# A decoder layer's recurrence: the tiled output products of eight chunks in one visit instead of two, and the output transposes six dense products later

## The chip, the cores and the metric

One core of a Trainium2 chip runs the kernel. A core has TensorE (PE, with its weight loads PEld), VectorE (DVE), ScalarE (ACT), GpSimd (POOL) and SyncE (SP), which here issues most of the DMAs. The engines run their own instruction lists and wait for one another through semaphores. TensorE writes to PSUM, eight banks of 128 partitions by 512 fp32 columns; all else lies in SBUF or in DRAM. The metric is the device time in microseconds, the median of several runs.

## The reference

One layer (DEPTH is 1) of a decoder trunk over 512 tokens of width 2048, all fp32:

```python
h = rms_norm(x, norm_g[i])
z = jnp.einsum('btd,dn->btn', h, w_in[i])     # r, k, v, lora inputs | gate | pool input | pool gate
...
def step(S, inp):                              # per head, 64 x 64 state
    sa = jnp.einsum('bhvk,bhk->bhv', S, -kk_t)
    S = S * w_t + sa * (kk_t * a_t) + v_t * k_t
    y_t = jnp.einsum('bhvk,bhk->bhv', S, r_t)
...
y = head_group_norm(y, ln_w[i], ln_b[i])       # per head and token, over 64 values
y_rwkv = (y + bonus) * jax.nn.silu(g_rwkv)
...                                            # pooled half, concat
x = x + jnp.einsum('btc,cd->btd', y_mix, w_out[i])
x = x + jax.nn.sigmoid(x @ w_pg[i] + b_pg[i]) * (p[i] @ w_ple[i])
return rms_norm(x, final_g)
```

The change concerns `y_t` for the 16 heads, the group norm behind it and the order of work around them.

## The kernel before

The large products (input projections, output projection, gate) are dense: weights and activations are split into a high and a low fp32r part (`wsplit`, `split`, L127 to L139: ScalarE casts the high part, VectorE subtracts), and three 128x128 by 128x512 matmuls per block of the contraction (`mm3`) stand for one fp32 product.

The recurrence goes by pairs of heads, j = 0 to 7, a pair filling 128 partitions, and by chunks of 64 tokens, ch = 0 to 7. Within a chunk the recurrence is turned into small matrix products. `recur(j, ...)` (L753) walks the eight chunks. A chunk has three hops on TensorE, each waiting for the one before through another engine:

- `py` (L781): the state block `sbd` of the chunk's start times the chunk's queries. It gives the state's part of the outputs, in one half of the rows, and the part that the next hop needs, in the other; VectorE adds `mv` to that other half and writes `zs` (L784).
- `pu` (L790): the inverted triangular block `x1` times `zs`. ScalarE copies the result into `uv` (L794).
- `ps` (L799): the keys `bkn` times `uv`, from which VectorE makes the next state block `sbd` (L804, L806).

A tile `py` is one PSUM bank and holds four chunks. The outputs also need products within the chunk, masked scores `mt` times `uv`. These are the tiled products: 64 output rows, 64 columns, the two chunks of an even-odd couple going to the two halves of the rows. They are added onto `py` eight calls at a time, after chunk 3 and after chunk 7; each call is two matmul instructions in the trace, so a visit has 16. ScalarE then copies the outputs of the four chunks from the bank to `ysb` (L827, two copies of 64x256). VectorE computes the group norm's statistics over `ysb` (L842, L844), a reciprocal square root in small steps (`rsqrt`, L142), and scales (L851).

Between the hops TensorE is kept busy with dense products. A generator `stream()` (L461) yields the dense work of the whole stage in a fixed order; `pump(n)` (L492) takes about n matmuls from it. `HC = (6, 9, 9)` (L867) are the amounts behind `py`, `pu` and `ps`.

`finish` (L854) is the end of a pair: four transposes of `ysb` to `pyt` (L858), ScalarE's scale and bias to `yo` (L860), two VectorE steps (L861, L862) and one DMA to the DRAM tensor `yd` (L863), issued by ScalarE. `yd` is read when the output projection starts. `finish` of pair j is put on the list `pending` and called while the next pair is prepared, in `gather(j + 1)` (L678); that of the last pair is called behind a pump of 40 (L902).

`gather(j)` runs between two pairs: decay and rate products `pu`, `pa` (L528, L543), transposes of v (`pv`, L688) and of the keys (`pbk`, L699), a pump of 8, the key norms `pss` (`norm_key`, L563), then the pumps and `finish` that the change touches, then the second half of the inversion: VectorE's transposes to `y1` (L723), the reciprocal of the key norms behind them (L572), and on TensorE `pq2`, `pmv` and `px2` (L728 to L741; the trace calls them pq, pmv, px), whose result completes `x1` (L745) for the next pair's first `pu`.

`scores(j + 1)` (L608) is called after chunk 0 of pair j. Its products `pm` need `bk` and `ar`, which VectorE makes in `prepare` (L577).

What sets the order: on TensorE every instruction of this stage is kept in program order (`pin`, L154 to L162). On the other engines a planner orders the instructions by priority and estimated times; `tc.high_priority` lifts those of the recurrence's hops, and `tc.issue_after` puts some behind others.

PSUM pools: `psY` has two banks under tag `y`, used in turn by `pv`, by two of the four `pm` tiles and by the `py` tiles. `psM` has three banks, for `pu`/`pa` of `decay_and_rate`, `pbk`, `pss`, `pyt`, `pq2`, `pmv`, `px2` and others. `psA` holds the dense accumulations, `psS` the `pu` and `ps` of the hops.

Of the kernel before, what the change touches and what calls it, by code (L numbers as in the profile page):

```python
# [9 lines left out]
F32 = mybir.dt.float32  # L10
# [5 lines left out]
P = 128  # L16
T = 512
# [7 lines left out]
NCH = T // C  # L25
# [9 lines left out]
def trunk_kernel(ctx: ExitStack, tc: tile.TileContext, x, p, norm_g, w_in, mu, w0, w_up, a0, a_up,  # L35
                 k_k, k_a, r_k, ln_w, ln_b, w_pool, pool_scale, w_out, w_ple, w_pg, b_pg, final_g, out):
    nc = tc.nc
# [118 lines left out]
    def mm(*a, **k):  # L156
        i = nc.tensor.matmul(*a, **k)  # L157
        return tc.keep_in_program_order(i) if pin[0] else i
# [333 lines left out]
    def pump(n):  # L492
        debt[0] += n
        while debt[0] > 0:
            c = next(big, None)
            if c is None:
                debt[0] = 0
                return
            debt[0] -= c
# [178 lines left out]
    def gather(j):  # L678
        d = st_[j]
        bk, v_, mt = d.pop("bk"), d.pop("v_"), d["mt"]  # L680
        if j + 1 < NJ:
            prepare_key(j + 1)
            decay_and_rate(j + 1)

        uv = rw.tile([P, NCH, P], F32, name=f"uv{j}", tag="uv")
        ps = psY.tile([P, T], F32, name=f"pv{j}", tag="y")
        for tt in range(NT):
            tr(ps[:, tt * P:(tt + 1) * P], v_[:, tt * P:(tt + 1) * P], ident)  # L688
        pv = ps.rearrange("p (t c) -> p t c", c=P)
        nc.scalar.copy(uv[0:64, 0::2, :], pv[0:64])  # L690
        nc.scalar.copy(uv[64:128, 1::2, :], pv[64:128])


        bkn = rw.tile([P, NCH, P], F32, name=f"bkn{j}", tag="bkn")
        for hf in range(2):
            ps = psM.tile([P, T], F32, name=f"pbk{j}_{hf}", tag="m")
            for i in range(4):
                ch = 4 * hf + i
                tr(ps[:, i * P:(i + 1) * P], bk[:, ch // 2, 2 * (ch % 2):2 * (ch % 2) + 2, :], ident)  # L699
            nc.scalar.copy(bkn[:, 4 * hf:4 * hf + 4, :], ps.rearrange("p (c n) -> p c n", n=P))  # L700

        pump(H4)

        d.update(uv=uv, bkn=bkn)
        if j + 1 < NJ:
            norm_key(j + 1)
        pump(H5)
        if pending:
            pending.pop()()
        pump(HX)  # L710

        x1 = d["x1"]

        def units(fn):
            for u in range(8):
                for par in range(2):
                    fn(u, par, 64 * (1 - par))

        y1 = rw.tile([P, 8, 32], F32, name=f"y1{j}", tag="tm")

        with tc.issue_after(late[0].ins):
            for pb in (0, 64):
                yt = nc.vector.transpose(y1[pb:pb + 32], x1[pb:pb + 32, :, 0:32])  # L723
        if j + 1 < NJ:
            with tc.issue_after(yt.ins):
                scale_key(j + 1)
        ps3 = psM.tile([P, 8, 32], F32, name=f"pq2{j}", tag="m")
        units(lambda u, par, pb: mm(ps3[pb + 32:pb + 64, u, :],  # L728
                                                  mt[pb:pb + 32, par, u, 1 - par, 32:64],
                                                  y1[pb:pb + 32, u, :], start=True, stop=True,  # L730
                                                  tile_position=(pb, pb + 32)))
        q2t = rw.tile([P, 8, 32], F32, name=f"q2{j}", tag="xw")
        with tc.high_priority(offset=HP):
            for pb in (0, 64):
                nc.scalar.copy(q2t[pb + 32:pb + 64], ps3[pb + 32:pb + 64])
        psv = psM.tile([P, 8, C], F32, name=f"pmv{j}", tag="m")
        units(lambda u, par, pb: mm(psv[pb:pb + 64, u, :], mt[64 - pb:128 - pb, par, u, 1 - par, :],
                                    uv[64 - pb:128 - pb, 2 * (u // 2) + par, 64 * (u % 2):64 * (u % 2) + 64],
                                    start=True, stop=True))
        ps4 = psM.tile([P, 8, 32], F32, name=f"px2{j}", tag="m")  # L740
        units(lambda u, par, pb: mm(ps4[pb:pb + 32, u, :], q2t[pb + 32:pb + 64, u, :],  # L741
                                                  x1[pb + 32:pb + 64, u, 32:64], start=True, stop=True,
                                                  tile_position=(pb + 32, pb)))
        for pb in (0, 64):
            nc.scalar.copy(x1[pb:pb + 32, :, 32:64], ps4[pb:pb + 32])  # L745
        mv = rw.tile([P, 4, P], F32, name=f"mv{j}", tag="mv")
        nc.scalar.copy(zsp[0][64:128, :].rearrange("p (h t) -> p h t", h=2), psv[64:128, 0:2, :])
        nc.scalar.copy(mv.rearrange("p q (h t) -> p (q h) t", h=2), psv)
        d["mv"] = mv
        pump(2 * H1)  # L750


    def recur(j, work, between):  # L753
# [13 lines left out]


        ysb = rw.tile([P, NT, P], F32, name=f"ysb{j}", tag="t", bufs=4)
        py = None  # L770
        for ch in range(NCH):
            par, q = ch % 2, ch // 2
            pb = 64 * (1 - par)
            cur, nxt = sbd[ch % 2], sbd[(ch + 1) % 2]
            pcc = pw[:, ch, C:C + 1]
            sl = slice((ch % 4) * P, (ch % 4 + 1) * P)
            if ch % 4 == 0:
                py = psY.tile([P, T], F32, name=f"py{j}_{ch}", tag="y")
            zs = zsp[par]
            if ch > 0:  # L780
                mm(py[:, sl], ar[:, q, 2 * par:2 * par + 2, :], cur, start=ch in (1, 4), stop=True,  # L781
                                 skip_group_check=True)
                with tc.high_priority(offset=HP):
                    lead[0] = nc.vector.tensor_tensor(zs[pb:pb + 64], py[pb:pb + 64, sl], mv[pb:pb + 64, q, :],  # L784
                                                      ALU.add)
                step()
                pump(HC1)

            psu = psS.tile([P, T], F32, name=f"pu{j}_{ch}", tag="s")
            mm(psu[:, 0:P], x1[:, 2 * q:2 * q + 2, :], zs, start=True, stop=True)  # L790
            for h in range(2):
                hc = slice(64 * h, 64 * h + 64)
                with tc.high_priority(offset=HP):
                    nc.scalar.copy(uv[pb:pb + 64, ch, hc], psu[hc, hc])  # L794
            step()
            pump(HC2)
            if ch < NCH - 1:
                pss = psS.tile([P, T], F32, name=f"ps{j}_{ch}", tag="s")
                mm(pss[:, 0:P], bkn[:, ch, :], uv[:, ch, :], start=True, stop=True)  # L799
                for h in range(2):  # L800
                    hc = slice(64 * h, 64 * h + 64)
                    with tc.high_priority(offset=HP):
                        if ch == 0:
                            lead[0] = nc.vector.tensor_scalar(nxt[hc, hc], pss[hc, hc], pcc[hc], None, ALU.mult)  # L804
                        else:
                            lead[0] = nc.vector.scalar_tensor_tensor(nxt[hc, hc], pss[hc, hc], pcc[hc], s0p[hc, :],  # L806
                                                                     ALU.mult, ALU.add)
                s0p = rw.tile([P, C], F32, name=f"s0p{j}_{ch}", tag="s0p", bufs=2)
                pcn = pw[:, ch + 1, C:C + 1]
                if ch < NCH - 2:  # L810
                    for h in range(2):
                        hc = slice(64 * h, 64 * h + 64)
                        nc.gpsimd.tensor_scalar(s0p[hc, :], nxt[hc, hc], pcn[hc], None, ALU.mult)  # L813
            if ch % 4 == 3:
                for qq in range(2):
                    for h in range(2):
                        for pr in range(2):
                            c_ = ch - 3 + 2 * qq + pr
                            yr = slice(64 * pr, 64 * pr + 64)
                            o_ = (2 * qq + pr) * P + 64 * h  # L820
                            mm(py[yr, o_:o_ + 64], mt[:, pr, 2 * (c_ // 2) + h, pr, :],
                                             uv[:, c_, 64 * h:64 * h + 64], start=False, stop=True,
                                             skip_group_check=True)
                py4 = py.rearrange("p (s c) -> p s c", c=P)
                for pr in range(2):
                    yr = slice(64 * pr, 64 * pr + 64)
                    nc.scalar.copy(ysb[yr, q - 1:q + 1, :], py4[yr, pr::2, :])  # L827
            step()
            if ch == 0:
                between()  # L830
            else:
                pump(HC3)
# [345 lines left out]
```

## Time and profile before

| what | value |
|---|---|
| median of three runs | 1095.2 us (1094.84 to 1095.33) |
| the profiled execution: its own time, and its span | 1094.06 us, 1092.3 us |
| granted TensorE clock, mean | 0.998 |
| busy in the span: PE, PEld, DVE, ACT, POOL | 1067.4, 879.1, 707.9, 448.2, 74.4 us |
| busy from 125 to 715 us, which holds the eight recurrences | PE 585.7, DVE 448.2, ACT 248.7 of 590 us |
| tiled products mt times uv | 256 matmul instructions, 16 a visit, 16 visits from 155.7 to 699.5 us |
| ysb copies | 32, median 367 ns |

A row of the time line gives the start, the length in us, engine, line, operation, output and inputs, shapes, the count of instructions merged in the row, and in brackets the engine's idle time before it with what ended it. A row of the chain of waits gives start, length and what; the chain is followed back from the last instruction to what released it. A row of the waits gives who waited for whom: the total, the number of times and the longest. Of TensorE the matmuls overlap, so the start of the next row, not the length, tells what one costs. A row by stretch has the stretch, its length, then busy us and count of PE, PEld, DVE, ACT and POOL, the granted clock, the DMA share and the GB/s.

### The profile page before, as it was taken

Reading aid. Unit: us, or ns where it says so; the run is one execution under the profiler, and the core shown is the slowest. Engines: PE = TensorE matmul, PEld = TensorE weight load, DVE = VectorE, ACT = ScalarE, POOL = GpSimd, SP = SyncE. Lnnn points to the kernel's source line nnn. Section 1 sums busy time; section 2 is a strip of 40 time slices with the busy share of each in tenths; the row PEclk is TensorE's granted clock in tenths of the full one; section 3 lists DMA queues with packets and bytes.
Section 4 is the critical chain, followed back from the end, with each engine's and each line's share of the span. In section 5 each row is a group of like instructions: output and inputs, shape, how many; then the busy total and the mean of one; then the engine's idle time right before and its main releaser. Section 6 shows DMA issues by size and latency. Waiting matters only on the chain.

```text
span 1092.3 us, 17194 instructions
## 1 busy us (share of the span) xinstructions
PE 1067.4 (98%) x6060; PEld 879.1 (80%) x6060; DVE 707.9 (65%) x1835; ACT 448.2 (41%) x917; POOL 74.4 (7%) x180
## 2 busy tenths in 40 slices
PE   5999999999999999999999999999999999999996
PEld 4888878888888888787888788888888888888885
DVE  6687867878779679678886956454433424445366
ACT  7633534435335335353443344544222222233337
POOL 2100010110110110100101101000000000000000
PEclk9999999999999999999999999999999999999999
DMA  7433433332423333333334242774534438454534
GB/s 233 116 97 97 112 92 79 102 101 72 127 81 102 105 91 89 95 83 90 94 93 120 79 138 94 231 242 163 171 123 141 164 97 261 129 187 147 174 105 154
DMA packets 178485, 138.56 MB, mean 127 GB/s; under 512 B 34677, under 2 KB 139742, under 8 KB 178398
## 3 DMA queue, kind: packets, MB, share of 16 engines
q1 hardware_dynamic: 157694, 103.89, 32.2%
q10 hardware_dynamic: 20704, 33.56, 9.5%
q8 instruction: 48, 0.79, 0.3%
q14 instruction: 39, 0.32, 0.1%
HBM read 118.02 MB, written 18.87 MB: 125 GB/s over the span
## 4 chain that ended last, share of the span: by engine, by line
PE 88%; DVE 5%; DMA 3%; ACT 2%; issue 1%; SPq 0%; ACTq 0%; DVEq 0%
PE acc_o L157 16%; PE acc_g L157 16%; PE zb L157 15%; PE zv L157 8%; PE zr L157 7%; PE zg L157 7%; PE zk L157 6%; DMA n<-nd 2%; PE py L157 2%; PE pple L157 2%; PE pu L157 2%; PE pm L157 1%; PE pp L157 1%; PE ps L157 1%; PE pmv L157 1%
## 5 line engine op out<-in xcount | busy, mean ns | idle before, releaser
L133 DVE TENSOR_TENSOR wlo_g<-raw_g,whi_g 128x512 fp32r<-128x512 f32 x84 | 56.9, 683 | 78.7 <-ACT whi_g L132 78.5
L157 PE MATMUL zb<-hhi,whi_b 128*128 128x512 f32 x256 | 106.3, 415 | 0.0
L133 DVE TENSOR_TENSOR wlo_o<-raw_o,whi_o 128x512 fp32r<-128x512 f32 x64 | 43.9, 690 | 92.3 <-ACT whi_o L132 92.2
L157 PE MATMUL zb<-hhi,wlo_b 128*128 128x512 f32 x256 | 100.5, 393 | 0.0
L157 PE MATMUL acc_o<-whi_o,ylo 128*128 128x512 f32 x256 | 100.2, 391 | 0.0
L157 PE MATMUL acc_o<-whi_o,yhi 128*128 128x512 f32 x256 | 99.9, 390 | 0.0
L157 PE MATMUL zb<-hlo,whi_b 128*128 128x512 f32 x256 | 99.8, 390 | 0.0
L157 PE MATMUL acc_o<-wlo_o,yhi 128*128 128x512 f32 x256 | 99.7, 389 | 0.0
L132 ACT CAST whi_g<-raw_g 128x512 fp32r<-128x512 f32 x84 | 51.9, 620 | 105.5 <-PE acc_g L157 60.3
L157 PE MATMUL acc_g<-whi_g,x2hi 128*128 128x512 f32 x208 | 81.2, 391 | 0.0
L157 PE MATMUL acc_g<-wlo_g,x2hi 128*128 128x512 f32 x208 | 81.0, 389 | 0.0
L157 PE MATMUL acc_g<-whi_g,x2lo 128*128 128x512 f32 x208 | 80.6, 389 | 0.0
L132 ACT CAST whi_o<-raw_o 128x512 fp32r<-128x512 f32 x64 | 39.9, 623 | 97.8 <-PE acc_o L157 97.8
L813 POOL TENSOR_SCALAR s0p<-sbd,pw 64x64 f32<-64x64 f32 x96 | 56.7, 590 | 338.5 <-DVE sbd L806 253.7
L132 ACT CAST whi_b<-raw_b 128x512 fp32r<-128x512 f32 x64 | 39.7, 620 | 87.1 <-PE zv L157 34.9
L133 DVE TENSOR_TENSOR wlo_b<-raw_b,whi_b 128x512 fp32r<-128x512 f32 x64 | 43.7, 684 | 34.2 <-ACT whi_b L132 33.0
L157 PEld LDWEIGHTS zb<-hhi,wlo_b 128*128 128x128 f32 x256 | 48.0, 188 | 11.0
L661 DVE TENSOR_TENSOR xw<-xw,tm 128x60 f32<-128x60 f32 (+24 forms) x248 | 51.9, 209 | 6.8
L157 PEld LDWEIGHTS acc_o<-wlo_o,yhi 128*128 128x128 f32 x256 | 48.1, 188 | 10.0
L157 PEld LDWEIGHTS acc_o<-whi_o,ylo 128*128 128x128 f32 x256 | 48.1, 188 | 9.9
L157 PEld LDWEIGHTS acc_o<-whi_o,yhi 128*128 128x128 f32 x256 | 48.1, 188 | 9.6
L157 PEld LDWEIGHTS zb<-hhi,whi_b 128*128 128x128 f32 x256 | 48.3, 189 | 8.4
(285 smaller groups left out, 2546.8 us busy)
## 6 DMA issues: line engine op xcount, KB each, us to landing
raw_b<-in_w_in_dram SPq DMA_DIRECT2D x64, 256.0 KB
raw_o<-in_w_out_dram SPq DMA_DIRECT2D x64, 256.0 KB
raw_g<-in_w_pg_dram SPq DMA_DIRECT2D x64, 256.0 KB
raw_k<-in_w_in_dram SPq DMA_DIRECT2D x32, 256.0 KB
raw_r<-in_w_in_dram SPq DMA_DIRECT2D x32, 256.0 KB
raw_v<-in_w_in_dram SPq DMA_DIRECT2D x32, 256.0 KB
raw_g<-in_w_in_dram SPq DMA_DIRECT2D x32, 256.0 KB
n<-nd SPq DMA_DIRECT2D x16, 256.0 KB
```

What stands on the lines that cost most here:

```text
L132: nc.scalar.copy(hi, raw)
L133: nc.vector.tensor_tensor(lo, raw, hi.bitcast(F32), ALU.subtract)
L157: i = nc.tensor.matmul(*a, **k)
L661: nc.vector.tensor_tensor(xw[:, 0:n_, s + 1:32], xw[:, 0:n_, s + 1:32], tm[:, 0:n_, 0:w_], ALU.add)
L813: nc.gpsimd.tensor_scalar(s0p[hc, :], nxt[hc, hc], pcn[hc], None, ALU.mult)
```

## The change

Both `py` tiles of a pair are kept until the last chunk. The visit behind chunk 3 goes; behind chunk 7 the eight calls for chunks 0 to 3 are issued, their two copies to `ysb`, then the eight for chunks 4 to 7 and their two copies. In `gather`, `finish` of the pair before is called after 19 pumped products instead of 13, and 7 follow instead of 13; the sum stays 26.

```diff
         if j + 1 < NJ:
             norm_key(j + 1)
-        pump(H5)
+        pump(H5 + 6)
         if pending:
             pending.pop()()
-        pump(HX)
+        pump(HX - 6)
...
-        py = None
+        pys = {}
...
             if ch % 4 == 0:
-                py = psY.tile([P, T], F32, name=f"py{j}_{ch}", tag="y")
+                pys[ch // 4] = psY.tile([P, T], F32, name=f"py{j}_{ch}", tag="y")
+            py = pys[ch // 4]
...
-            if ch % 4 == 3:
-                for qq in range(2):
-                    for h in range(2):
-                        for pr in range(2):
-                            c_ = ch - 3 + 2 * qq + pr
...
-                            mm(py[yr, o_:o_ + 64], mt[:, pr, 2 * (c_ // 2) + h, pr, :],
-                                             uv[:, c_, 64 * h:64 * h + 64], start=False, stop=True,
-                                             skip_group_check=True)
-                py4 = py.rearrange("p (s c) -> p s c", c=P)
-                for pr in range(2):
-                    yr = slice(64 * pr, 64 * pr + 64)
-                    nc.scalar.copy(ysb[yr, q - 1:q + 1, :], py4[yr, pr::2, :])
+            if ch == NCH - 1:
+                for c0 in range(0, NCH, 4):
+                    py = pys[c0 // 4]
+                    for qq in range(2):
+                        for h in range(2):
+                            for pr in range(2):
+                                c_ = c0 + 2 * qq + pr
...
+                                mm(py[yr, o_:o_ + 64], mt[:, pr, 2 * (c_ // 2) + h, pr, :],
+                                   uv[:, c_, 64 * h:64 * h + 64], start=False, stop=True, skip_group_check=True)
+                    py4 = py.rearrange("p (s c) -> p s c", c=P)
+                    for pr in range(2):
+                        yr = slice(64 * pr, 64 * pr + 64)
+                        nc.scalar.copy(ysb[yr, c0 // 2:c0 // 2 + 2, :], py4[yr, pr::2, :])
             step()
```

More of the change, by code (lines that the diff above doesn't have):

```diff
@@ L813, in recur @@
                         nc.gpsimd.tensor_scalar(s0p[hc, :], nxt[hc, hc], pcn[hc], None, ALU.mult)
-            if ch % 4 == 3:
-                for qq in range(2):
-                    for h in range(2):
-                        for pr in range(2):
-                            c_ = ch - 3 + 2 * qq + pr
-                            yr = slice(64 * pr, 64 * pr + 64)
-                            o_ = (2 * qq + pr) * P + 64 * h
-                            mm(py[yr, o_:o_ + 64], mt[:, pr, 2 * (c_ // 2) + h, pr, :],
-                                             uv[:, c_, 64 * h:64 * h + 64], start=False, stop=True,
-                                             skip_group_check=True)
-                py4 = py.rearrange("p (s c) -> p s c", c=P)
-                for pr in range(2):
-                    yr = slice(64 * pr, 64 * pr + 64)
-                    nc.scalar.copy(ysb[yr, q - 1:q + 1, :], py4[yr, pr::2, :])
+            if ch == NCH - 1:
[6 more added lines that the diff above has]
+                                yr = slice(64 * pr, 64 * pr + 64)
+                                o_ = (2 * qq + pr) * P + 64 * h
+                                mm(py[yr, o_:o_ + 64], mt[:, pr, 2 * (c_ // 2) + h, pr, :],
+                                   uv[:, c_, 64 * h:64 * h + 64], start=False, stop=True, skip_group_check=True)
+                    py4 = py.rearrange("p (s c) -> p s c", c=P)
+                    for pr in range(2):
+                        yr = slice(64 * pr, 64 * pr + 64)
+                        nc.scalar.copy(ysb[yr, c0 // 2:c0 // 2 + 2, :], py4[yr, pr::2, :])
             step()
```

## The prediction

> **What bounds the kernel now.** I read the page first, then the busy time by stretch, then the chain of waits from 200 to 300 us, and last the time lines of the engines around one pair's end.
>
> ```profile
> PE 1067.4 (98%) x6060; PEld 879.1 (80%) x6060; DVE 707.9 (65%) x1835; ACT 448.2 (41%) x917; POOL 74.4 (7%) x180
> ...
> PE 88%; DVE 5%; DMA 3%; ACT 2%; issue 1%; SPq 0%; ACTq 0%; DVEq 0%
> ```
>
> ```profile
> 125.00:715.00 590.00, 585.70 (x3723) 479.58 (x3722) 448.22 (x1344) 248.71 (x541) 64.02 (x114) 1.00 0.37 104
> ```
>
> TensorE is busy 98% of the span and 88% of the chain that ended last. In the stretch that holds all eight pairs it is busy 585.7 of 590.0 us at full granted clock. What sets the end there is the length of TensorE's instruction list, whose order the code pins; time is won by shortening that list and lost where another engine is late for an entry of it. VectorE, at 448 of 590 us, is the engine that can be late. Those waits are few:
>
> ```profile
> PEld py L157 <- DVE sbd L806: 5.9, 9, 1.0
> PEld pu L157 <- DVE zs L784: 3.4, 6, 0.9
> ...
> PEld pu L157 <- ACT x L745: 2.0, 2, 1.4
> ```
>
> **The visits.** The tiled products come 16 at a time, once behind chunk 3 and once behind chunk 7. This is the chain of waits (start, length, what), with one ordinary hop, the chunk 3 visit, the chunk 7 visit and, at its end, two longer tiled visits of another kind:
>
> ```profile
> 223.29 0.22 PE ps L157 x2
> 223.51 2.08 PE zk L157 x9
> 225.59 0.22 PE py L157 x2
> ...
> 229.51 0.22 PE ps L157 x2
> 229.73 0.62 PE py L157 x16
> 230.34 2.27 PE zk L157 x9
> 232.61 0.22 PE py L157 x2
> ...
> 253.08 2.09 PE zv L157 x9
> 255.17 0.61 PE py L157 x16
> 255.79 2.28 PE zv L157 x9
> 258.07 0.46 PE pu L157 x2
> ...
> 269.68 0.62 PE pq L157 x32
> 270.30 1.08 PE pmv L157 x32
> ```
>
> An ordinary hop, from ps to py, takes 225.59 - 223.29 = 2.30 us. With the visit it takes 232.61 - 229.51 = 3.10. So the visit costs 0.80 us, and 0.18 of that is not in its own row: the nine dense products behind it take 2.27 in place of 2.09. The chunk 7 visit costs the same: 258.07 - 253.08 = 4.99 against two runs of nine, 4.17, is 0.82.
>
> The change takes the first visit away and appends its 16 products to the second. What do 16 products cost inside a visit already open? No row shows 32 of this shape. Below: pq does 32 small ones in 0.62, as long as our 16, so the appended ones could cost almost nothing and the whole 0.80 be won (8 x 0.80 = 6.4 us). Above: a full visit again, 0.80, nothing won. The nearest row is pmv, which like ours streams 64 columns into 64 output rows: 32 in 1.08, which is 0.46 more than our 16. I take 0.46, so each pair saves 0.80 - 0.46 = 0.34 us, and eight pairs 2.7 us. The matmuls, 256 in all, stay the same; what goes is the entry to and exit from tiled work, once per pair.
>
> **The cover that the first visit gave.** Behind chunk 3, VectorE had 3.10 us to make the next state block sbd before py needs it; now it has 2.30, like every other hop. In a pair where sbd was among the latest after that visit:
>
> ```profile
> 304.05 0.23 PE ps L157 x2
> ```
>
> ```profile
> 305.29 0.29 DVE L806 SCALAR_TENSOR_TENSOR sbd<-ps,pw,s0p 64x64 f32<-64x64 f32 x1
> ```
>
> sbd ends at 305.58, which is 1.53 after ps, and 0.77 before the new deadline. I cost it at nothing; without this slack it would be at most the 0.80 that the hop loses.
>
> **The evacuation at the pair's end.** Four ysb copies instead of two now run on ScalarE behind chunk 7, and eight bn_stats instead of four on VectorE. The rows for the pair that ends at 255 us, ScalarE, VectorE and TensorE in turn:
>
> ```profile
> 255.86 0.75 ACT L827 COPY ysb<-py 64x256 f32<-64x256 f32 x2 [0.96 <-PE py L157]
> 257.92 0.62 ACT L132 CAST whi_b<-raw_b 128x512 fp32r<-128x512 f32 x1 [1.31 <-issue]
> ```
>
> ```profile
> 256.64 0.61 DVE L842 BATCH_NORM_STATS2 st<-ysb 128x6 f32<-128x64 f32 x4 [1.01 <-ACT ysb L827]
> ...
> 265.16 0.30 DVE L851 TENSOR_SCALAR ysb<-ysb,mvr,rs 128x64 f32<-128x64 f32 x1
> 265.38 0.68 DVE L568 TENSOR_SCALAR kk<-pss 128x512 f32<-128x512 f32 x1
> 265.98 0.89 DVE L723 STREAM_TRANSPOSE y<-x 32x256 f32<-32x256 f32 x2
> 266.90 3.35 DVE L572 RECIPROCAL kk<-kk 128x512 f32<-128x512 f32 x1
> ```
>
> ```profile
> 258.82 0.60 PE L161 MATMUL pv<-ident,sv 128*128 128x128 f32 x4
> ...
> 265.63 0.60 PE L161 MATMUL pyt<-ident,ysb 128*128 128x128 f32 x4
> ...
> 269.61 0.69 PE L157 MATMUL pq<-y,mt 32*32 32x32 f32 x32
> ```
>
> ScalarE: two more copies are 0.75 us, ending at about 257.36. ScalarE stands idle for 1.31 us behind them now, so the next weight split at 257.92 isn't late; if a planned split filled that gap, it would be late by 0.75. Both PSUM banks of the py tag are now held to this point, and pv needs one: at 258.82 plus 0.46, it is 1.9 us behind the last copy. Cost nothing; a bank held past that point would stall TensorE by the same amount.
>
> VectorE: the four moved bn_stats (0.61) fall in while it waits for the extra copies, so the chain of norms ends about 0.75 later. TensorE itself is 0.46 later by then, so net lateness is 0.29 us. The first user is pyt: the last norm ends at 265.46, pyt starts at 265.63, a slack of 0.17 that would turn negative. This is where the second part of the change acts: six dense products of 0.23 move pyt back by 1.39, and the slack becomes 0.17 - 0.29 + 1.39 = 1.27. The move adds and removes no product, since the following pump gets six fewer. Queued behind the norms on VectorE are kk<-pss, the two y transposes and the 3.35 us reciprocal. pq needs y: 266.87 against 269.61, a slack of 2.74 that becomes 2.45. The scaling yo and its two VectorE steps follow pyt; they ran behind the reciprocal anyway (end 270.25), and yo's one write to memory, from ScalarE's queue, is read only after the last pair. SP's queue of weight loads is not touched, and nothing waits on POOL for it.
>
> The lateness of 0.29 bites where VectorE has no slack. Two places:
>
> ```profile
> 430.96 0.73 DVE L600 TENSOR_TENSOR bk<-kk,ipw 128x512 f32<-128x512 f32 x1
> ```
>
> ```profile
> 431.91 2.06 PE L157 MATMUL pm<-ar,bk 64*128 64x128 f32 x32
> ```
>
> ```profile
> 491.90 1.75 DVE kk L572
> ...
> 499.79 0.37 ACT x L745
> 500.20 0.49 PE pu L157 x2
> ```
>
> bk ends at 431.69, 0.22 ahead of pm: 0.07 is lost there. Before 500.20 the chain runs from that reciprocal on VectorE and ScalarE to pu: the full 0.29 is lost. Together 0.36 us. Against it, the first half's statistics no longer sit on VectorE in the middle of the recurrence:
>
> ```profile
> 307.26 0.26 DVE st L842 x2
> ```
>
> This row lies on the chain that leads to a late sbd. I put its gain at the same 0.36, of the 5.9 us of such waits, and let the two cancel; the bounds are 0 and a few of these waits of up to 1.0 each.
>
> **The sum.** -6.4 (eight first visits) + 3.7 (appended products) + 0.36 - 0.36 = -2.7 us. The profiled execution has a span of 1092.3 us and a time of 1094.06, 1.1 below the median of the runs, 1095.2. From its own time the sum gives 1091.4; against the median, which is what is measured, **1092.5 us**.
>
> **The rivals.**
>
> *The order is drawn anew and stalls elsewhere (about 1095).* Only TensorE's order is pinned; VectorE's and ScalarE's are planned from estimated times, and new lengths make a new plan. The three wait rows above sum to 11.3 us in 17 waits; four more of the mean 0.66 cost 2.7 and end at 1095.2. For it: such waits appear at irregular places from pair to pair. Against it: a redraw can as well remove some.
>
> *VectorE's tail becomes the bound (slower).* Place: from the last ysb copy through norms, transposes and reciprocal to pu. If copies (0.75) and statistics (0.61) fall in series, the tail is 1.36 later, less 0.46 is 0.90 per pair; where every pair has as little slack as the one before 500.20, seven pairs lose 6.3, net +3.6, 1098.8. It decides once the slack at pq, pm and pu is under 0.5 in at least six pairs; the rows show that only in two, with 2.74 at pq. [...]
>
> *The joined visit saves nothing.* If each bank of 16 has its own entry cost, the appended products cost 0.80 and the time stays at 1095.2. Against it: pmv's 32 and pq's 32 in single rows.
>
> *More is won.* If the two removed blocks (copies and statistics in mid-chain) end three of the waits on sbd, at 0.66 each, 2.0 more is won: 1090.5.
>
> **How the numbers follow.** Forecast 0.50, new order 0.22, VectorE's tail 0.10, nothing saved 0.08, more won 0.10. What a measurement here can tell from no change is about 0.2%, 2.2 us. The forecast is 0.5 beyond it, so I give 0.43 of its 0.50 to faster and 0.07 to no change. New order: 0.17 no change, 0.05 slower. Tail: slower. That makes faster 0.53, no change 0.32, slower 0.15. The range goes from 1090.0, a little below the case of more won, to 1096.0, the new order with one wait more; outside lie the tail, the worst of the new orders and a little below, 0.17.
>
> **What would show it.** One py run of 32 in about 1.08 us per pair, followed by nine dense in about 2.28; ps to py behind chunk 3 at 2.30; pv without a wait; the last norm ahead of pyt by about a microsecond; pm and pu late by at most 0.3 more. I am wrong if the run of 32 takes 1.4 or more, if pv, pyt or pq wait in most pairs, or if waits on sbd, zs and x sum to much more than 11.3 us.

## The result, and the profile after

| | before | changed |
|---|---|---|
| median of five runs | 1095.2 us (1094.63 to 1096.03) | 1108.55 us (1107.71 to 1111.86) |
| profiled execution: time, span | 1094.06, 1092.3 us | 1108.52, 1106.8 us |
| granted TensorE clock, mean | 0.998 | 0.992 |

The ratio is 1.0125, with an interval of 1.0114 to 1.0136: the change makes the kernel 13.4 us slower, where the forecast was 2.7 us faster. The time lies far outside the range of 1090.0 to 1096.0.

The busy times of the changed kernel's page, and its row for the stretch from 125 to 715 us (busy us and count of PE, PEld, DVE, ACT and POOL, granted clock, DMA share, GB/s):

```profile
PE 1071.9 (97%) x6060; PEld 881.3 (80%) x6060; DVE 707.6 (64%) x1835; ACT 448.5 (41%) x917; POOL 71.7 (6%) x180
```

```profile
125.00:715.00 590.00, 575.87 (x3659) 469.70 (x3658) 437.27 (x1299) 241.56 (x527) 61.82 (x114) 0.99 0.35 99
```

The counts of instructions are those of before, and VectorE's busy time is the same to 0.3 us. No work was added. TensorE, which before was busy for 585.7 of the 590 us, is now busy for 575.9 and does fewer matmuls in them: it stands still. What it waits for stands at the top of its waits (who waited for whom: total, times, longest):

```profile
PE pyt L161 <- DVE ysb L853: 9.2, 5, 4.5
...
PE py L157 <- DVE sbd L807: 3.1, 3, 1.3
...
PE pu L157 <- DVE zs L785: 0.7, 2, 0.4
```

The first row has no counterpart before. The output transposes wait for the norms' scaling (L853, which was L851). Six dense products were put ahead of them so that they would not.

Where the loss arises, pair by pair, shows in the start of the first dense product behind each pair's last visit of tiled products. Those starts, read from both time lines:

| pair's end | before, us | changed, us | lag | grown by |
|---|---|---|---|---|
| 0 | 181.76 | 181.45 | -0.31 | |
| 1 | 255.72 | 255.86 | +0.14 | 0.45 |
| 2 | 330.84 | 336.46 | +5.62 | 5.48 |
| 3 | 406.35 | 418.74 | +12.39 | 6.77 |
| 4 | 480.20 | 494.30 | +14.10 | 1.71 |
| 5 | 555.03 | 569.80 | +14.77 | 0.67 |
| 6 | 631.58 | 646.34 | +14.76 | -0.01 |
| 7 | 699.65 | 714.07 | +14.42 | -0.34 |

In pair 0, ahead of the first wait of pyt, the changed kernel is ahead by 0.31, and over pair 7 it gains 0.34: the gain that was forecast for each pair. But 12.25 of the 14.4 us come between the ends of pairs 1 and 3. Those are the two places where the outputs of pair 1 and pair 2 are finished. This is TensorE's time line at the first of them:

```profile
254.78 1.15 PE L157 MATMUL py<-uv,mt 128*64 128x64 f32 x32
255.86 0.50 PE L157 MATMUL zv<-hhi,whi_v 128*128 128x512 f32 x1
...
258.97 0.60 PE L161 MATMUL pv<-ident,sv 128*128 128x128 f32 x4
...
266.90 0.39 PE L157 MATMUL zb<-hhi,wlo_b 128*128 128x512 f32 x1
270.63 1.72 PE L161 MATMUL pyt<-ident,ysb 128*128 128x128 f32 x4 [3.34 <-DVE ysb L853]
272.01 0.78 PE L157 MATMUL zb<-hhi,whi_b 128*128 128x512 f32 x1
272.58 0.63 PE L157 MATMUL zb<-hlo,whi_b 128*128 128x512 f32 x1
273.01 0.63 PE L157 MATMUL zb<-hhi,wlo_b 128*128 128x512 f32 x1
...
276.12 1.06 PE L157 MATMUL pq<-y,mt 32*32 32x32 f32 x32
```

The visit of 32 takes 255.86 - 254.78 = 1.08 us, and pv doesn't wait: the joined visit itself is as forecast. Then pyt waits 3.34 us, and behind the wait the dense products start 0.43 us apart (272.58 to 273.01) where they started 0.23 apart before. The granted clock tells why. Four stretches of the changed kernel around that wait:

```profile
255.00:266.00 11.00, 10.97 (x82) 9.10 (x78) 9.95 (x41) 8.89 (x20) 0.00 (x0) 1.00 0.29 67
266.00:270.60 4.60, 1.29 (x6) 0.75 (x4) 4.57 (x7) 0.62 (x1) 0.00 (x0) 0.99 0.20 57
270.60:276.80 6.20, 6.17 (x39) 4.15 (x41) 4.79 (x12) 1.39 (x2) 0.00 (x0) 0.50 0.15 42
276.80:290.00 13.20, 13.20 (x131) 10.90 (x127) 7.71 (x15) 6.21 (x14) 1.34 (x3) 0.98 0.43 129
```

For 6.2 us behind the wait, TensorE runs at a clock of 0.50, which costs it half of that, 3.1 us. Pair 2 is the same with a longer wait:

```profile
352.14 1.72 PE L161 MATMUL pyt<-ident,ysb 128*128 128x128 f32 x4 [4.50 <-DVE ysb L853]
```

```profile
352.10:357.00 4.90, 4.80 (x23) 3.19 (x25) 4.79 (x12) 0.78 (x1) 0.00 (x0) 0.65 0.28 85
```

There the slow clock costs 0.35 of 4.9, 1.7 us. The two waits (7.84) and the two slow stretches (4.8) make 12.6 us, against a lag grown by 12.25 from which two joined visits have taken 0.7: 12.9.

Why the norms are late is seen on VectorE. Its time line in the changed kernel, behind the same visit:

```profile
256.29 0.61 DVE L844 BATCH_NORM_STATS2 st<-ysb 128x6 f32<-128x64 f32 x4 [0.98 <-ACT ysb L829]
...
257.71 0.60 DVE L844 BATCH_NORM_STATS2 st<-ysb 128x6 f32<-128x64 f32 x4
...
258.62 0.17 DVE L849 TENSOR_SCALAR ve<-mvr 128x8 f32<-128x8 f32 x1
258.74 0.69 DVE L133 TENSOR_TENSOR wlo_b<-raw_b,whi_b 128x512 fp32r<-128x512 f32 x1
259.34 0.16 DVE L143 TENSOR_SCALAR rs<-ve 128x8 int32<-128x8 int32 x1
259.43 0.75 DVE L370 SCALAR_TENSOR_TENSOR sv<-zv,prm,sv 128x511 f32<-128x511 f32 x1
260.10 0.16 DVE L144 TENSOR_SCALAR ve<-ve 128x8 f32<-128x8 f32 x1
...
266.07 0.17 DVE L151 SCALAR_TENSOR_TENSOR rs<-nt,rs 128x8 f32<-128x8 f32 x1
266.15 3.35 DVE L572 RECIPROCAL kk<-kk 128x512 f32<-128x512 f32 x1
269.42 0.63 DVE L133 TENSOR_TENSOR wlo_g<-raw_g,whi_g 128x512 fp32r<-128x512 f32 x1
269.96 1.86 DVE L853 TENSOR_SCALAR ysb<-ysb,mvr,rs 128x64 f32<-128x64 f32 x8
```

And the kernel before at the same place:

```profile
257.56 0.17 DVE L847 TENSOR_SCALAR ve<-mvr 128x8 f32<-128x8 f32 x1
257.76 0.17 DVE L143 TENSOR_SCALAR rs<-ve 128x8 int32<-128x8 int32 x1
257.97 0.17 DVE L144 TENSOR_SCALAR ve<-ve 128x8 f32<-128x8 f32 x1
...
262.84 0.16 DVE L151 SCALAR_TENSOR_TENSOR rs<-nt,rs 128x8 f32<-128x8 f32 x1
```

Between the statistics and the scaling lies the reciprocal square root: with the step that prepares it, twelve steps of 128x8, each of which must follow the one before. Before, the first six ran one behind the other, 0.2 us apart, and the chain took from 257.56 to 263.00, 5.4 us. Now there is a full-size operation between every two steps, and it takes from 258.62 to 266.24, 7.6 us. It ends 3.2 us later, though it began only 1.1 later. (The two more copies alone are 0.75; ScalarE also did a cast of 0.62 us for the key norms between the first two and the last two, at 256.28, and these ended at 257.68.) And when it ends, the reciprocal of the key norms (3.35 us) stands in VectorE's list ahead of the scaling: the last norm ends at 269.96 + 1.86 = 271.82, where it ended at 265.46.

VectorE's time lines show the reciprocal (L572) ahead of the norms in exactly pairs 1 and 2 of the changed kernel, and in no pair of the kernel before.

### The profile page after: what moved, and what is told of

Its sections match the earlier page's. It is cut to its first block, busy times and chain, and to the rows that moved or that the text cites. A ratio compares the mean times of both kernels' runs of the same rounds, so it can differ in the third digit from the quotient of the medians.

```text
span 1106.8 us, 17193 instructions
## 1 busy us (share of the span) xinstructions
PE 1071.9 (97%) x6060; PEld 881.3 (80%) x6060; DVE 707.6 (64%) x1835; ACT 448.5 (41%) x917; POOL 71.7 (6%) x180
```

## The experiments

Two theories were open. By the *order theory*, the joined visit starts the chain of small steps later, the planner fills in full-size work between its steps and puts the reciprocal ahead of the scaling, and all of the loss is the wait at pyt with what follows it. By the *move theory*, it is the second part of the change that hurts: pyt and what lies behind it come later. Four kernels were run on one chip, beside the kernel before at 1094.45 us.

**The joined visit without the later transposes.** Against the changed kernel:

```diff
-        pump(H5 + 6)
+        pump(H5)
...
-        pump(HX - 6)
+        pump(HX)
```

> The joined visit alone, the output transposes where they were before. Theory (order): with the joined visit the norm steps become ready so late that the plan puts the 3.35 us reciprocal ahead of them in two pairs; the transposes then wait, and 1.39 us longer than in the changed kernel in each of the six pairs that wait there: about 1108.6 + 8 = 1117 us (1113 to 1119). Rival (move): the delayed transposes are what made the plan put the norms late; without the move the time is 1093 to 1096 us.

Measured: 1115.22 us (1113.16 to 1117.92), ratio 1.019 [1.017, 1.021]. Its waits:

```profile
PE pyt L161 <- DVE ysb L853: 13.9, 8, 5.3
```

The joined visit alone is slower still, and waits longer at pyt. The six products ahead of pyt win about 7 us (20.8 above the kernel before against 13.4); they cover a part of the wait and no more.

**The later transposes without the joined visit.** Against the kernel before:

```diff
-        pump(H5)
+        pump(H5 + 6)
...
-        pump(HX)
+        pump(HX - 6)
```

> Two visits as before, the output transposes six dense products later. Order theory: nothing on TensorE is added and the norms stay ahead of the reciprocal; 1095 us, within 1093.5 to 1096.5. Rival (move): 1102 us or more, with waits of pyt on ysb.

Measured: 1094.39 us (1093.62 to 1096.52), ratio 1.0002 [0.9993, 1.0011], and pyt doesn't wait. The move theory falls: the second part of the change costs nothing.

**The reciprocal behind the norms.** Against the changed kernel, the key norms' scaling, reciprocal first, is put behind the last norm of the pair before:

```diff
-            nc.vector.tensor_scalar(y8[:, i, :], ...)
+            normed[0] = nc.vector.tensor_scalar(y8[:, i, :], ...)
...
-                scale_key(j + 1)
+                if normed[0] is None:
+                    scale_key(j + 1)
+                else:
+                    with tc.issue_after(normed[0].ins):
+                        scale_key(j + 1)
```

> The changed kernel with one thing more: the reciprocal of the key norms is issued behind the last norm scaling of the pair before. Order theory: in the two pairs with the large waits the norms end some 3.4 us earlier, the wait of pyt falls from 2.9 and 4.7 us to about 1, and with it the half clock behind it goes: 1108.6 - 10 to 1108.6 - 11, that is 1097 to 1099 us. Rival (amount): VectorE has too much to do at the pair's end whatever the order, and the wait goes to pq or pu: 1106 to 1110 us.

Measured: 1099.99 us (1096.71 to 1103.18), ratio 1.0051 [1.0039, 1.0064]. From VectorE's time line, TensorE's waits, and the stretch around pair 1's pyt:

```profile
266.48 1.20 DVE L858 TENSOR_SCALAR ysb<-ysb,mvr,rs 128x64 f32<-128x64 f32 x5
...
268.19 0.76 DVE L858 TENSOR_SCALAR ysb<-ysb,mvr,rs 128x64 f32<-128x64 f32 x3
268.86 3.35 DVE L573 RECIPROCAL kk<-kk 128x512 f32<-128x512 f32 x1
```

```profile
PE pyt L161 <- DVE ysb L858: 4.1, 6, 1.3
```

```profile
264.00:278.00 14.00, 12.97 (x143) 10.06 (x142) 13.49 (x27) 6.29 (x16) 0.40 (x1) 1.00 0.25 76
```

The norms end at 268.95 in place of 271.82, the longest wait is 1.3 us in place of 4.5, and the clock stays at 1.00. (The expectation's 2.9 and 4.7 us are the waits of 3.34 and 4.50 us above.) The place of the reciprocal is thus worth some 8 us of the loss. The rest, 5.5 us, stays: the chain is still pulled apart, and pyt waits in six places. The time is about a microsecond above what was expected, and the runs scatter over 6.5 us where those of the kernel before scatter over 3.4. The one profile is of the shortest run, which had the mean granted clock of the kernel before, 0.998. The three longest runs, of 1101.08 to 1103.18 us, had 0.994 or 0.995. There the clock fell too, and 0.3% to 0.4% of the time is 3 to 4 us, an estimate; which waits it fell behind was not seen.

**The transposes thirteen products later.** Against the changed kernel, H5 + 13 and HX - 13 in place of H5 + 6 and HX - 6.

> The changed kernel with the output transposes 13 dense products later instead of 6, that is with all 26 ahead of them. Order theory: the norms end when they did, so each wait of pyt shrinks by up to 7 x 0.23 = 1.6 us (0.7, 1.6, 1.6, 1.6, 0.7 and 0.2 in the six pairs): about 1102 us (1100 to 1104). Rival: the wait is handed on to the tiled products behind, which need the same engine: 1107 to 1109 us.

Measured: 1101.64 us (1099.88 to 1102.95), ratio 1.0063 [1.0048, 1.0078]; pyt waits 4.4 us in three places, the longest 2.5. Seven more products of cover take 6 us off, as expected. They come off the idle time: by the busy times of the pages TensorE is idle for 28.9 us of the span in place of 34.9, and busy for as long as in the changed kernel (1072.0 and 1071.9 us). The slow clock, which the expectation left out, is still there behind the shorter waits. This is pair 2, from TensorE's time line and by stretch:

```profile
350.56 1.58 PE L161 MATMUL pyt<-ident,ysb 128*128 128x128 f32 x4 [2.47 <-DVE ysb L853]
```

```profile
353.00:360.40 7.40, 7.40 (x75) 6.10 (x71) 4.93 (x10) 4.42 (x10) 0.50 (x1) 0.54 0.24 76
```

In pair 1, where pyt waits 1.30 and 0.66 us with one transpose between, the stretch from 271.0 to 278.4 has 0.54 too. The two stretches cost 0.46 of 14.8, 6.8 us, no less than those of the changed kernel.

If the chain is the cause, then a shorter one must cure the changed kernel and a longer one must hurt the kernel before, with its two visits untouched. The next four ran beside the kernel before at 1095.47 us.

**A shorter chain.** Against the changed kernel, the group norm's reciprocal square root takes one refinement step in place of three, which leaves out six of the chain's small instructions per pair and a part of the computation's accuracy:

```diff
-        for _ in range(3):
+        for _ in range(steps):
...
-        rsqrt(rs8, ve8, nt8)
+        rsqrt(rs8, ve8, nt8, 1)
```

> The changed kernel with a shorter chain: the group norm's reciprocal square root does one Newton step instead of three, six small VectorE steps fewer per pair (it leaves out that refinement; all other work is there). Order theory: the norms are ready before the reciprocal in every pair, pyt doesn't wait, and the joined visit's gain shows: 1092.5 us (1091 to 1094). Rival (copies): the two more copies and four more statistics make the norms late whatever the chain's length; 1099 us or more.

Measured: 1091.37 us (1090.29 to 1093.14), ratio 0.9963 [0.9948, 0.9977]; pyt doesn't wait. The instructions left out are 48 of VectorE's 1835, 4.7 us of its 707.6 busy, on an engine with time to spare. Without them the changed kernel is some 17 us faster: in a list that is served in order each of them was a turn in the queue, and now the norms come ahead of the reciprocal in every pair. Both parts of the change are in this kernel, so together they cost nothing that shows where the norms are in time. The kernel before was not run with one step, so how much of the 4.1 us below it is owed to the shorter chain itself stays open here.

**A longer chain, with two visits.** Against the kernel before, five refinement steps in place of three.

> The kernel before, two visits and the transposes in their old place, with five Newton steps instead of three: six small VectorE steps more per pair, some 1 us of work. Order theory: a longer chain alone is enough; the plan then puts the norms behind the reciprocal in four pairs, and with 6 to 7 us in each of them the time is 1115 to 1125 us. Rival (joined visit): the wait comes from the four copies in one place, and without them six steps cost what they take, 1095 to 1098 us.

Measured: 1132.88 us (1132.25 to 1134.19), ratio 1.034 [1.0308, 1.0373]. TensorE's waits, and VectorE's time line behind pair 1:

```profile
PE pyt L161 <- DVE ysb L851: 23.6, 7, 6.0
```

```profile
271.00 0.17 DVE L150 TENSOR_TENSOR nt<-nt,rs 128x8 f32<-128x8 f32 x1
271.08 3.35 DVE L572 RECIPROCAL kk<-kk 128x512 f32<-128x512 f32 x1
274.34 0.10 DVE L151 SCALAR_TENSOR_TENSOR rs<-nt,rs 128x8 f32<-128x8 f32 x1
...
274.96 1.87 DVE L851 TENSOR_SCALAR ysb<-ysb,mvr,rs 128x64 f32<-128x64 f32 x8
```

The direction is the order theory's: a chain that is late is overtaken by the reciprocal, here ahead of its last step, without any joined visit. The size isn't: more than the expected 1115 to 1125. The norms stand behind the reciprocal in four pairs, as expected, but the expectation priced the idle time alone. That is 23.6 us at pyt; most of the other 14 us goes with the clock, which was at 0.50 behind waits of five pairs and in the mean at 0.983 in place of 0.998.

**The chain on GpSimd.** Against the changed kernel, all steps of the reciprocal square root but the first run on GpSimd, where the last operation of each refinement becomes two:

```diff
-            nc.vector.scalar_tensor_tensor(y, t, 1.5, y, ALU.add, ALU.mult)
+            nc.gpsimd.tensor_scalar(t, t, 1.5, None, ALU.add)
+            nc.gpsimd.tensor_tensor(y, t, y, ALU.mult)
```

> The changed kernel with the chain of small steps (all but the first integer step) on GpSimd, which is idle there. Order theory: nothing goes between the steps any more, the norms are ready before the reciprocal, and the time is that of the forecast, 1092.5 us (1091 to 1094), if a GpSimd step on 128x8 takes up to 0.3 us; at 0.6 us, the time of its 64x64 step, the chain is again 8 us long and the time is 1096 us or more. Rival (amount): VectorE's backlog remains without those steps; 1099 us or more.

Measured: 1108.36 us (1107.34 to 1109.9), ratio 1.012 [1.0092, 1.0147], a miss. The wait at pyt is nearly gone, and another has come. From TensorE's waits, and VectorE's time line behind pair 1:

```profile
PE pu L162 <- ACT x L750: 9.2, 5, 3.4
...
PE pyt L166 <- DVE ysb L858: 0.8, 1, 0.8
```

```profile
267.89 1.88 DVE L858 TENSOR_SCALAR ysb<-ysb,mvr,rs 128x64 f32<-128x64 f32 x8 [2.69 <-POOL rs L154]
```

The planner now puts the norms early, ahead of the reciprocal, as was wanted. But GpSimd isn't done when VectorE reaches them, and VectorE stands idle for 2.69 us with the next pair's work queued behind. That lateness reaches the next pair's first pu by way of ScalarE. Behind the reciprocal VectorE has the last step of the pair's output yo (L869), which ends at 278.38. ScalarE stands idle for 3.48 us until then, since the DMA of yo, which it issues, stands in its list ahead of its copies, x among them. So x starts at 279.54, 3.3 us after its product px has ended (276.21). The clock fell here as well, to a mean of 0.994. The same mechanism, one station on: an instruction placed too early in an in-order list holds up what is behind it, as one placed too late holds up its user.

**The reciprocal behind the norms, and the transposes thirteen products later.** The edits of the third and the fourth kernel together.

> The changed kernel with the reciprocal behind the norms, and the transposes 13 dense products later instead of 6. The waits that the third run left at pyt (1.1, 2.1, 3.3, 2.4, 1.1, 0.6 and 0.3 us) shrink by up to 1.6 each: about 2.5 us are left, 1094.5 us (1093 to 1096), about the time before. Rival: pq, just behind, waits for the same engine; 1098 us or more.

Measured: 1092.13 us (1088.77 to 1092.89), ratio 0.9964 [0.995, 0.9979]. (The expectation's waits sum to 10.9 us and the third kernel's view of the waits has 4.1 at pyt: the view counts idle time alone, and the four transposes of a pair also stand further apart.) To learn whether the joined visit brings this, or the two edits by themselves, they were put on both kernels and run beside the kernel before at 1094.46 us.

**The same two edits with two visits:**

> The kernel before, with two visits, but with the two other parts of the eighth run: the reciprocal behind the norms and the transposes 13 dense products later. If the joined visit alone makes the eighth run faster, this one is as the kernel before, 1095 us, within 0.15%. Rival (the order does it): 1092 us, as the eighth run.

Measured: 1094.93 us (1092.83 to 1097.25), ratio 1.0003 [0.9994, 1.0013].

**And again with the joined visit:**

> The eighth run's kernel once more, beside its counterpart with two visits on the same chip: 8 x 0.34 = 2.7 us less than that, some of it given to waits left at pyt; 1.5 to 3.5 us less.

Measured: 1092.11 us (1089.74 to 1094.14), ratio 0.9982 [0.9973, 0.9992]. VectorE's and TensorE's time lines behind pair 1:

```profile
265.18 1.20 DVE L858 TENSOR_SCALAR ysb<-ysb,mvr,rs 128x64 f32<-128x64 f32 x5
...
266.89 0.75 DVE L858 TENSOR_SCALAR ysb<-ysb,mvr,rs 128x64 f32<-128x64 f32 x3
267.56 3.34 DVE L573 RECIPROCAL kk<-kk 128x512 f32<-128x512 f32 x1
```

```profile
267.59 0.60 PE L161 MATMUL pyt<-ident,ysb 128*128 128x128 f32 x4
268.12 0.69 PE L157 MATMUL pq<-y,mt 32*32 32x32 f32 x32
```

The norms end at 267.64 and the transposes start without a wait. With the two other edits in both kernels, the joined visit is worth 1094.93 - 1092.11 = 2.8 us; the intervals of the two ratios, 0.9994 to 1.0013 and 0.9973 to 0.9992, just don't meet. Taken together they leave about 1.5 us of doubt either way. This is the version that beats both kernels, by 0.2% to 0.4% of the kernel before in its two series.

## Why the prediction was wrong, step by step

- **The visits: right.** The visit of 32 takes 1.08 us from its start to the next dense product; 16 took 0.61 (255.17 to 255.79 in the prediction's chain of waits). The appended products cost 0.47, where 0.46 was put. Pair 0 ends 0.31 earlier, pair 7 gains 0.34, and 2.8 us in the whole are measured where the two sums of the visits gave 2.7. The 0.46 was read from a row of another shape, so that it came out to 0.01 is in part luck, and the 2.8 is known to about 1.5 us only.
- **The cover that the first visit gave: right.** Behind chunk 3, ps to py is 2.30 us (229.83 to 232.13 in pair 1). TensorE's three waits on sbd, 3.1 us, come at other hops, ahead of chunk 3's own py in pairs 3, 4 and 5.
- **ScalarE's copies and PSUM: right but for the order.** The waits of TensorE have no row for pv, which starts at 258.97, 3.1 us behind the visit. But the copies end at 257.68, not at 257.36, though the visit starts 0.3 earlier: the plan put a cast between them. The prediction had thought of such a thing only for the gap behind the copies, and its 0.75 for the chain has no room for it.
- **The moved transposes: half right.** By themselves they cost nothing, as put. But their six products were to leave a slack of 1.27 us, and the norms were 3 to 4.5 us late on top.
- **The step that failed** is "the chain of norms ends about 0.75 later". Measured, the last norm ends at 271.82 in place of 265.46: 6.36 later. The prediction took VectorE's order of before and shifted it by the work that was added. That order isn't fixed; it is planned. The small steps, started 1.1 us later, met other work that was ready, and got a full-size operation between every two of them (2.2 us more of chain); and the reciprocal, which the prediction had queued *behind* the norms, came ahead of them (3.35 us, with the weight split behind it). Why the planner chose so can only be argued, from the chain's later start: no run shows its estimates.
- **The two terms of 0.36: not seen.** The changed kernel has no wait on bk for pm and none on x for pu, and the gain on sbd didn't come: the matmuls waited for it 3.1 us in place of 1.9, the weight loads 7.1 in place of 5.9. No run tells why.
- **What follows a wait had no price.** The prediction costed lateness as idle time alone. Behind waits of 3.34 and 4.50 us TensorE also ran at a lower clock, which cost 4.8 us more in the two pairs.
- **The rivals.** "The order is drawn anew" named the cause, but priced it as four more waits of the usual length, 2.7 us; it should have asked which long operation can change places with which short one, and 3.35 us stood in a quoted row. "VectorE's tail becomes the bound" had the right side and the right place, but a sum of lengths as its mechanism, and looked for the waits at pq, pm and pu; they came at pyt, in two pairs for the most part, not at a steady 0.90 in each of seven. Its 0.10 and the 0.05 of the new order's slow side were too little.
- **Of the signs named beforehand**, the run of 32, ps to py and pv came out as put. The waits of the weight loads on sbd and zs, 11.3 us with those on x before, sum to 10.1, in these rows of the changed kernel's waits, where none on x is left. (They overlap matmuls, so they are not all lost time; the matmuls' own waits for the three were 3.6 us before and are 3.8 now.)

```profile
PEld py L157 <- DVE sbd L807: 7.1, 10, 1.7
...
PEld pu L157 <- DVE zs L785: 3.0, 5, 0.9
```

The one that failed, "the last norm ahead of pyt by about a microsecond", is the one that decided the time.

## What to carry to other kernels

A chain of small dependent steps on an engine that works its list in order costs as many turns in the queue as it has steps, and what a planner puts between them sets its length (here 5.4 us before and 7.6 us in the changed kernel for the same twelve steps): price it by the operations that may come between, and don't shift the old order by the added work. Where the engine's list holds one long operation, ask for each result that the bottleneck waits for whether that operation can come ahead of it, and put it behind by an explicit order; with that and enough cover, the joined visit is worth what it saves, here 2.8 us. Price idle time on TensorE above its length: in these runs the mean granted clock was 0.54 behind a wait of 2.47 us at pyt, 0.50 behind one of 3.34 and 0.65 behind one of 4.50, and it fell behind some shorter waits too.

## What the runs showed of the hardware

The granted clock fell behind the longest waits at pyt. In the changed kernel it was 0.50 for 6.2 us behind 3.34 us of idle time, and a mean of 0.65 over 4.9 us behind 4.50 us; dense products started 0.43 us apart in place of 0.23. In the profiled run of the kernel with the reciprocal behind the norms, where the longest wait was 1.3 us, the stretch around pair 1's pyt kept a clock of 1.00. In the kernel with the transposes thirteen products later, a wait of 2.47 us, with four transposes behind it, was followed by a mean clock of 0.54 over 7.4 us, and two waits of 1.30 and 0.66 us around one transpose by the same. And of two waits of nearly the same length it fell to 0.50 behind the one, 1.76 us at 433.03 in the kernel with the joined visit alone, and stayed at 1.00 behind the other, 1.80 us at 520.90 in the kernel with the longer chain. So the length of a single wait doesn't decide alone; what else counts was not tested.

GpSimd took 0.20 to 0.24 us for a 128x8 step for which VectorE takes 0.16 to 0.17, as this view of the operations of the kernel with the chain on GpSimd shows (min, median and max in ns, first and last start):

```profile
L150 POOL TENSOR_TENSOR nt<-rs,ve x24: 201/202/1071, 185.8 to 723.2; 128x8 f32<-128x8 f32 x24
```

The steps are thus a little dearer there by their medians; in the refinements at 265.61 us they start 0.28 to 0.31 us apart, where VectorE's start 0.20 apart when nothing comes between, and there are four to a refinement in place of three. What cost more is that VectorE waited for these steps, and ScalarE and TensorE for VectorE.
